# A hybrid decoder layer on one core: four edits, at the start, in the selection of experts, at the hand-over to v and in the final norm

## The chip, the cores and the metric

The kernel runs on one core of one Trainium2 chip. The metric is the device time of one execution in microseconds (us). The core has TensorE (PE, matmuls; PEld is its weight load), VectorE (DVE), ScalarE (ACT), GpSimd (POOL) and SyncE (SP), which here only issues DMAs. Each engine takes its instructions in the order in which they are written, and waits on semaphores for the others. A queue that issues DMAs does the same: a DMA that has to wait holds up all that stand behind it on its issuer.

## The reference

One trunk layer for 512 tokens of 1024 columns in float32:

```python
h = x + W_out [ GLA_group(n) ; SSD_group(n) ],   n = RMSNorm(x)
h = h + PEER(RMSNorm(h))
y = RMSNorm_final(h)
```

PEER is a retrieval of experts: per token 8 heads choose 16 of 16384 experts each by product keys, then

```python
act = jnp.einsum('td,ted->te', x_blk, u[i_blk])
hid = jax.nn.gelu(act, approximate=False) * g_blk
return jnp.einsum('te,ted->td', hid, v[i_blk])
```

## The kernel before, in words

The order of the work is written out by hand: the program sets no schedule of its own, so what stands first in the code stands first on its engine.

**Precision.** Most products are done in three matmuls (`mm3`, L106): an operand is split into a rounded high part, made by ACT, and the rest, made by DVE or POOL (`split`, L102), and high by high, high by low and low by high are added in PSUM (L108, L109, L110).

**Mixers** (`mixers`, L132). The four token tiles of x are loaded, squared, scaled by their norm (`scale`, L237), transposed on PE (L266), and evicted from PSUM as high part `nT` (ACT) and low part (DVE). Then the blocks of the input projection follow. `ahead` (L158) loads and splits weight blocks ahead of their use; raw blocks are `wraw`, split ones `b`. The first blocks' low parts are made by POOL.

**U steps.** PEER is done densely for three of the four token tiles (384 tokens, `TD`): for each of 128 blocks e of 128 experts, PE computes u of the block times the tokens (a U step: 8 parts of 3 matmuls of 384 columns, `u_part`, L1050), ACT applies gelu, and the result is kept in `ring`, 59 rows of 384 tokens. The raw block of u, `ur` (two buffers), is loaded by SP and split in two halves, one half-step ahead (`rhs_part`, L839). Before the gates are there, the halves' low parts `ul` are made by POOL, from `hold` on by DVE. The fourth tile's experts are gathered row by row by indirect DMAs (`gather`).

**Selection** (from L1086). While U steps run on PE, DVE picks the best experts: `select(t)` (L976) resolves token tile t to expert numbers with float16 comparisons and sums over `gat`; `ties(t)` (L962) lets ACT write four pieces of a helper tile `k` inside the following U steps, at parts 1 and 5; two tiles of `k` serve four t, so the pieces of t+2 wait until `select(t)` has read its last. `spread(t)` (L1013) transposes the numbers and the gates of tile t on PE, `spread2(t)` (L1022) moves them to float16. `u_run(n)` stands for n U steps.

**Gates** (from L1214). 48 units of 8 tokens each: DVE builds one-hot tiles `A`, `eq`, `B`, PE multiplies them (L1186), and the gates go by ACT and DVE to `ring` (rows that exist) or by ACT to `stage`, which every 8 units is written to DRAM, `gd`, by a DMA of ACT's queue (L1199). Between the units U parts are spread evenly: `parts = 8 * (RS - LEFT - nu[0])`, so that 57 U steps are done at the end, whatever number was done before.

**Hand-over and loop over v** (from L1230). The pool of the gates (`gp`) is closed and the pool of v (`vp`) opened on the same bytes: its raw buffers `vr` lie where `stage` lay. Then comes the loop over e (L1322): per turn 6 groups of 3 matmuls of 512 columns (v of block e times the ring row e, accumulated in 6 PSUM banks), one U step, two or one gathers, the loads of the next `vr`, `ur` and, once a row is used, of `ring` from `gd` (`gload`, L1251). From row 59 on the gate is in the ring row before the U step's result is multiplied into it by DVE (`keep`, L1036).

**Final norm** (`final`, L1257). For each tile the residual is added from PSUM (DVE), squared halfwise (ACT), the mean (two short DVE instructions) goes to POOL for the power -0.5, and the result is scaled by that and by the norm's weight.

Of the kernel before, what the change touches and what calls it, by code (L numbers as in the profile page):

```python
# [7 lines left out]
F32 = mybir.dt.float32  # L8
F32R = mybir.dt.float32r
# [9 lines left out]
D = 1024  # L19
# [16 lines left out]
class Stream:  # L36
# [10 lines left out]
    def loads(s, upto):  # L47
        while s.nl <= min(upto, len(s.src) - 1):
            s.raw[s.nl] = s.c.tile([128, 1024], F32, name=s.nm + "r", bufs=s.nraw)
            s.y.load(s.raw[s.nl], s.src[s.nl])  # L50
            s.nl += 1
# [12 lines left out]
class Layer:  # L64
# [67 lines left out]
    def mixers(self):  # L132
# [125 lines left out]
        scale(2, 1, False)  # L258
        scale(3, 0, True)
# [7 lines left out]
        for dc in range(8):  # L267
            if dc == 0:
                ahead(0, 3, 0)
            act(nh[dc], px[dc], AF.Copy, scale=wmix[:, dc:dc + 1])  # L270
            stt(nl[dc], px[dc], wmix[:, dc:dc + 1], nh[dc].bitcast(F32), OP.mult, OP.subtract)
            if dc == 4:
                ahead(0, 3, 1)
# [584 lines left out]
    def experts(self):  # L858
# [237 lines left out]
        select(1)  # L1096
        spread(0)
        u_run(1)
# [10 lines left out]
        u_run(4)  # L1109
# [124 lines left out]
        vs.loads(1)  # L1234
# [4 lines left out]
        vs.loads(3)  # L1239
# [15 lines left out]
        gload(RS)  # L1255

        def final():  # L1257
# [3 lines left out]
            junk = [c.tile([128, D], F32, name="gat", tag="gat", bufs=3), vp.tile([128, D], F32, name="vr", bufs=4)]  # L1261
# [26 lines left out]
            def scale(t):  # L1288
                stt(hs[t], hs[t], v[t][:, 3:4], wf, OP.mult, OP.mult)
                load(self.out[t], hs[t])  # L1290
# [9 lines left out]
            scale(3)  # L1300
            mean(0)
            power(0)
            residual(1, 0)
            weight(1, 0, G)
            residual(1, 1)
            weight(1, 1, G)
            scale(0)
            mean(1)
            power(1)
            residual(2, 0)  # L1310
            weight(2, 0, G)
            residual(2, 1)
            weight(2, 1, V)
            act(hs[1], hs[1], AF.Copy, scale=v[1][:, 3:4])
            load(self.out[1], hs[1])
            mean(2)
            power(2)
            act(hs[2][:, hf[0]], hs[2][:, hf[0]], AF.Copy, scale=v[2][:, 3:4])
            V.tensor_scalar(hs[2][:, hf[1]], hs[2][:, hf[1]], v[2][:, 3:4], None, op0=OP.mult)
            load(self.out[2], hs[2])  # L1320

        for e in range(NE):  # L1322
# [8 lines left out]
            vs.loads(e + 4)  # L1331
# [15 lines left out]
            for i in range(3):  # L1347
                vgrp(0, i)
                if i == 2:
# [3 lines left out]
                    gload(e + 1 + RS)  # L1353
# [3 lines left out]
            for i in range(3):  # L1357
# [5 lines left out]
                fill(3 + i)  # L1363
            u_part(7)
            fill(6)
            if e == NE - 12:
                for t in (0, 1):
                    hs[t] = us.c.tile([128, D], F32, name="ur", bufs=2)
# [100 lines left out]
```

## Time and profile before

| what | before |
|---|---|
| median of 3 runs | 1508.53 us |
| lowest and highest of them | 1506.76 and 1512.19 us |
| the profiled execution, its time | 1503.02 us |
| span of the profiled execution, first to last instruction | 1501.2 us |
| busy share of the span: PE, DVE, ACT, POOL | 97%, 78%, 42%, 30% |
| DMA: mean rate over the span | 224 GB/s |

The profiled execution's own time is 1.8 us longer than its span, which is launch and end around it; it lies 0.4% under the median of the three runs. Engines work side by side, so a busy share says little by itself: what counts is where PE, the busiest engine, stands still, and what ended each stop. A matmul row gives the start and the modelled duration; matmuls are pipelined, so the pace is read from start to start. In the rows further below, the bracket at the end is the engine's idle time before the instruction and what ended it.

### The profile page before, as it was taken

How to read it: one execution, taken by the hardware profiler on the slowest of the kernel's cores; microseconds unless marked ns; L12 is line 12 of the kernel's file. 1: busy time of each engine (PE TensorE's matmuls, PEld its weight loads, DVE VectorE, ACT ScalarE, POOL GpSimd, SP SyncE). 2: the span in 40 equal slices, each digit the busy share in tenths (PEclk: the TensorE clock that was granted, in tenths of full speed). 3: DMA queues.
4: the chain of work that ended last, by engine and by line, in shares of the span. 5: the costliest groups of instructions: out<-in, count | busy, mean ns of one | idle time of the engine just before them, and what ended most of it. 6: DMA issues, size and time to landing. Idle time of an engine off the chain costs nothing.

```text
span 1501.2 us, 22402 instructions
## 1 busy us (share of the span) xinstructions
PE 1456.2 (97%) x7904; PEld 1278.0 (85%) x7904; DVE 1169.4 (78%) x2473; ACT 632.7 (42%) x1201; POOL 451.7 (30%) x380
## 2 busy tenths in 40 slices
PE   7999999999898999979999999999999999999997
PEld 5787778888898999878999999999999998888886
DVE  6542663789999999967877778777788888888886
ACT  5435633433654544433333333333333333444444
POOL 2002404444672000002333333333333333333332
PEclk9999999999999999999999999999999999999999
DMA  5231224222334556658888888889899888888894
GB/s 189 84 126 58 71 73 155 96 85 85 105 104 143 159 167 175 180 181 300 322 316 316 323 312 307 317 305 332 304 331 322 314 316 276 292 300 299 297 325 178
DMA packets 148738, 335.56 MB, mean 224 GB/s; under 512 B 64640, under 2 KB 73872, under 8 KB 148496
## 3 DMA queue, kind: packets, MB, share of 16 engines
q1 hardware_dynamic: 58672, 186.32, 36.1%
q0 software_dynamic: 36864, 134.23, 25.1%
q10 hardware_dynamic: 53088, 13.57, 3.9%
q8 instruction: 62, 1.02, 0.3%
q14 instruction: 52, 0.43, 0.1%
HBM read 315.79 MB, written 18.28 MB: 223 GB/s over the span
## 4 chain that ended last, share of the span: by engine, by line
PE 80%; DVE 12%; issue 3%; DMA 2%; ACT 2%; POOL 0%; SPq 0%; DVEq 0%; POOLq 0%; ACTq 0%
PE pm L109 25%; PE pm L108 25%; PE pm L110 25%; DVE gat L97 4%; PE pg L1186 2%; DVE B L97 1%; DVE ul L104 1%; PE pm L904 1%; DMA gd<-stage 1%; DVE ring L97 1%; DMA ur<-in_uT 1%; DVE eq L97 1%; DVE A L97 1%; ACT b L91 0%; ACT tp L91 0%
## 5 line engine op out<-in xcount | busy, mean ns | idle before, releaser
L108 PE MATMUL pm<-nT,uh 128*128 128x384 f32 (+1 forms) x1152 | 402.1, 349 | 8.8 <-ACT uh L91 8.3
L110 PE MATMUL pm<-nT,ul 128*128 128x384 f32 (+1 forms) x1152 | 397.0, 345 | 2.0 <-POOL ul L104 2.0
L109 PE MATMUL pm<-nT,uh 128*128 128x384 f32 (+1 forms) x1152 | 397.0, 345 | 0.5 <-DVE nT L97 0.5
L109 PE MATMUL pm<-vl,hh 128*128 128x512 f32 x765 | 300.4, 393 | 0.2 <-DVE vl L104 0.2
L110 PE MATMUL pm<-vh,hl 128*128 128x512 f32 x765 | 300.3, 393 | 0.0
L108 PE MATMUL pm<-vh,hh 128*128 128x512 f32 x765 | 299.0, 391 | 0.2 <-ACT vh L91 0.2
L1135 POOL DMA_INDIRECT gat<-in_u,idx x128 | 136.8, 1069 | 473.3 <-DVE gat L100 467.0
L91 ACT ACTIVATE uh<-ur 128x512 fp32r<-128x512 f32 x288 | 180.2, 629 | 214.1 <-PE pm L109 182.0
L108 PEld LDWEIGHTS pm<-nT,uh 128*128 128x128 f32 x1152 | 218.1, 189 | 33.5 <-ACT uh L91 8.7
L109 PEld LDWEIGHTS pm<-nT,uh 128*128 128x128 f32 x1152 | 218.1, 189 | 25.0 <-DVE nT L97 1.1
L110 PEld LDWEIGHTS pm<-nT,ul 128*128 128x128 f32 x1152 | 217.7, 189 | 9.1 <-POOL ul L104 2.9
L1135 POOL DMA_INDIRECT gat<-in_v,idx x128 | 147.2, 1150 | 253.1 <-DVE n2a L100 220.4
L91 ACT ACTIVATE vh<-vr 128x512 fp32r<-128x512 f32 x255 | 159.4, 626 | 136.8 <-PE pm L110 135.4
L104 DVE TENSOR_TENSOR vl<-vr,vh 128x512 fp32r<-128x512 f32 x255 | 175.3, 688 | 37.4 <-ACT vh L91 36.4
L104 DVE TENSOR_TENSOR ul<-ur,uh 128x512 fp32r<-128x512 f32 x206 | 140.7, 689 | 56.8 <-ACT uh L91 56.4
L100 DVE SCALAR_TENSOR_TENSOR n2a<-gat,dots,n2a 128x1024 f32<-128x1024 f32 x128 | 164.0, 1281 | 21.5 <-DMA gat<-in_v,idx 18.5
L110 PEld LDWEIGHTS pm<-vh,hl 128*128 128x128 f32 x765 | 143.7, 188 | 30.9
L100 DVE SCALAR_TENSOR_TENSOR gat<-gat,n2a 128x1024 f32<-128x1024 f32 x128 | 156.2, 1220 | 9.8 <-DMA gat<-in_u,idx 9.6
L108 PEld LDWEIGHTS pm<-vh,hh 128*128 128x128 f32 x765 | 144.0, 188 | 14.2 <-ACT vh L91 0.7
L109 PEld LDWEIGHTS pm<-vl,hh 128*128 128x128 f32 x765 | 144.0, 188 | 14.1 <-DVE vl L104 0.5
L104 POOL TENSOR_TENSOR ul<-ur,uh 128x512 fp32r<-128x512 f32 x82 | 118.7, 1455 | 99.8 <-ACT uh L91 99.4
L91 ACT ACTIVATE gl<-pm 128x384 f32<-128x384 f32 (+16 forms) x104 | 46.0, 442 | 219.8 <-PE pm L110 219.8
(254 smaller groups left out, 1685.2 us busy)
## 6 DMA issues: line engine op xcount, KB each, us to landing
ur<-in_uT SPq DMA_DIRECT2D x128, 512.0 KB, 6.0
vr<-in_v SPq DMA_DIRECT2D x128, 512.0 KB, 5.0
gd<-stage ACTq DMA_DIRECT2D x6, 2208.0 KB, 14.5
ring<-gd SPq DMA_DIRECT2D x69, 192.0 KB, 5.2
wraw<-in_w_in SPq DMA_DIRECT2D x23, 512.0 KB, 4.4
ur<-in_w_query SPq DMA_DIRECT2D x16, 512.0 KB, 3.7
b<-in_x SPq DMA_DIRECT2D x8, 512.0 KB, 3.6
wraw<-in_w_out SPq DMA_DIRECT2D x8, 512.0 KB, 3.9
```

What stands on the lines that cost most here:

```text
L91: return self.S.activation(out, in_, f, **k)
L97: return self.V.tensor_tensor(out, x, y, op=op)
L100: return self.V.scalar_tensor_tensor(out, x, s, y, op0=op0, op1=op1, **k)
L104: (self.G if pool else self.V).tensor_tensor(lo, src, hi.bitcast(F32), op=OP.subtract)
L108: T.matmul(out, lhi, rhi, start=start, stop=False)
L109: T.matmul(out, lhi, rlo, start=False, stop=False)
L110: T.matmul(out, llo, rhi, start=False, stop=stop)
L904: T.matmul(p[:, t * 128:(t + 1) * 128], q[:, t * 128:(t + 1) * 128], skT[:, b, :], start=True, stop=True)
L1135: G.indirect_dma_start(out=r, out_offset=None, in_=src, in_offset=bass.IndirectOffsetOnAxis(ap=idx[:, k:k + 1], axis=0))
L1186: T.matmul(o, A[:, t // 2, :, t % 2], B[:, i, t // 2, :, t % 2], start=i == 0, stop=i == 1)
```

## The change

The change has four parts.

1. Raw buffers. The buffers of a `Stream` (raw u and raw v) get a name each (`ur0`, `ur1`, `vr0` to `vr3`) where one name with several buffers stood. With that the four buffers of v are taken in the order in which they are first loaded, in rising addresses: `vr0` to `vr2` lie in the bytes of the one `stage` buffer, `vr3` across its border to the other. Three blocks of v are loaded ahead of the loop where four were, in one go; the fourth with the two next in turn 1. The loads of ring rows 59 and 60 from `gd` move from ahead of the loop and from turn 0's start to the end of turn 0.
2. Selection. `spread(0)` stands behind two U steps where it stood behind none, and one U step stood after it; the last run of U steps has five in place of four. In all 20 U steps lie in this stretch where 18 lay, and two fewer in the gates.
3. Start. The first weight block is split ahead of the last scaling of x, in halves, its low part by POOL; the third `wraw` load ahead stands one eviction later.
4. Final norm. Scalings are halved and put in another order, two multiplications by the weight on POOL fall away, and the last tile's output goes out in two halves, from ACT's and from SP's queue.

```diff
@@ Stream.loads
-            s.raw[s.nl] = s.c.tile([128, 1024], F32, name=s.nm + "r", bufs=s.nraw)
+            s.raw[s.nl] = s.c.tile([128, 1024], F32, name=f"{s.nm}r{s.nl % s.nraw}", bufs=1)
@@ mixers
         scale(2, 1, False)
+        parts[0] = b4(F32R), b4(F32R)
+        for k in range(2):
+            f = slice(k * 512, k * 512 + 512)
+            act(parts[0][0][:, f], raws[0][:, f], AF.Copy)
+        for k in range(2):
+            f = slice(k * 512, k * 512 + 512)
+            self.G.tensor_tensor(parts[0][1][:, f], raws[0][:, f], parts[0][0][:, f].bitcast(F32), op=OP.subtract)
+        raws.pop(0)
+        seen[1] = 1
         scale(3, 0, True)
...
-            if dc == 0:
+            if dc == 1:
                 ahead(0, 3, 0)
@@ experts, selection
         select(1)
+        u_run(2)
         spread(0)
-        u_run(1)
         ties(3)
...
         spread(2)
-        u_run(4)
+        u_run(5)
         spread2(2)
@@ experts, hand-over
-        vs.loads(1)
+        vs.loads(2)
         u_run(1)
         vs.split(1)
         hprep(0)
         u_run(1)
-        vs.loads(3)
...
-        gload(RS)
@@ final
...
             residual(1, 0)
             weight(1, 0, G)
+            scale(0, hf[0])
             residual(1, 1)
-            weight(1, 1, G)
-            scale(0)
+            residual(2, 0)
+            scale(0, hf[1])
+            load(self.out[0], hs[0])
+            residual(2, 1)
             mean(1)
             power(1)
-            residual(2, 0)
-            weight(2, 0, G)
-            residual(2, 1)
-            weight(2, 1, V)
-            act(hs[1], hs[1], AF.Copy, scale=v[1][:, 3:4])
-            load(self.out[1], hs[1])
+            scale(1, hf[1])
             mean(2)
             power(2)
+            act(hs[1][:, hf[0]], hs[1][:, hf[0]], AF.Copy, scale=v[1][:, 3:4])
+            load(self.out[1], hs[1])
+            weight(2, 0, V)
             act(hs[2][:, hf[0]], hs[2][:, hf[0]], AF.Copy, scale=v[2][:, 3:4])
-            V.tensor_scalar(hs[2][:, hf[1]], hs[2][:, hf[1]], v[2][:, 3:4], None, op0=OP.mult)
-            load(self.out[2], hs[2])
+            self.S.dma_start(self.out[2][:, hf[0]], hs[2][:, hf[0]])
+            scale(2, hf[1])
+            load(self.out[2][:, hf[1]], hs[2][:, hf[1]])
@@ experts, loop over e
-            vs.loads(e + 4)
+            vs.loads(e + 4 if e else 2)
...
-                    gload(e + 1 + RS)
+                    if e:
+                        gload(e + 1 + RS)
...
+            if e == 0:
+                gload(RS)
+                gload(RS + 1)
             u_part(7)
```

SP's queue at the hand-over, before. `vr` are raw blocks of v, `ur` of u, `ring<-gd` rows of gates; the brackets name the semaphores that a DMA waits for.

```order
L88 DMA vr_6961<-in_v 128x1024 [waits DMAHW6_49,PE_49]
L88 DMA vr_6963<-in_v 128x1024 [waits DMAHW4_49,Activation_49]
L88 DMA ur_6966<-in_uT 128x1024 [waits DMAHW2_49,DVE_49]
L88 DMA ur_7012<-in_uT 128x1024 [waits DMAHW3_49,DVE_49]
L88 DMA vr_7049<-in_v 128x1024
L88 DMA vr_7051<-in_v 128x1024
L88 DMA ring_2196<-gd_64 128x384 [waits DVE_49]
```

The same place in the change:

```order
L88 DMA vr0_6957<-in_v 128x1024 [waits DMAHW6_49,PE_49]
L88 DMA vr1_6959<-in_v 128x1024
L88 DMA vr2_6961<-in_v 128x1024
L88 DMA ur1_6964<-in_uT 128x1024 [waits DMAHW2_49,DVE_49]
L88 DMA ur0_7010<-in_uT 128x1024 [waits DMAHW3_49,DVE_49]
L88 DMA ur1_7061<-in_uT 128x1024 [waits DMAHW0_49,DVE_49]
L88 DMA ring_2198<-gd_64 128x384 [waits DMAHW4_49]
```

The wait for DMAHW4 stood on the second load of v, ahead of two loads of u; now it stands on the first ring row, behind three loads of v and three of u.

ACT's queue in the selection around `spread(0)`, before. A row `ring<-pm` ends a U step, `uh` are halves of u, `k8` pieces of `ties`, `gs` belongs to `spread(0)`.

```order
L91 ACTIVATE ring_2196<-pm_3859 128x384 [waits PE_49]
L91 ACTIVATE gs_2210<-pm_3912 128x128 [waits PE_49]
L91 ACTIVATE uh_3920<-ur_3860 128x512 [waits DMAHW2_49,Pool_49]
L91 ACTIVATE k8_3858<-tif_2205 128x1024
L91 ACTIVATE uh_3937<-ur_3860 128x512 [waits PE_49,Pool_49]
L91 ACTIVATE k8_3858<-tif_2205 128x1024
L91 ACTIVATE ring_2196<-pm_3917 128x384 [waits PE_49]
L91 ACTIVATE uh_3974<-ur_3918 128x512 [waits DMAHW3_49,Pool_49]
L91 ACTIVATE k8_3955<-tif_2205 128x1024 [waits DVE_49]
L91 ACTIVATE uh_3991<-ur_3918 128x512 [waits PE_49,Pool_49]
```

In the change:

```order
L91 ACTIVATE ring_2198<-pm_3861 128x384 [waits PE_49]
L91 ACTIVATE uh_3917<-ur1_3862 128x512 [waits DMAHW2_49,Pool_49]
L91 ACTIVATE k8_3860<-tif_2207 128x1024
L91 ACTIVATE uh_3934<-ur1_3862 128x512 [waits PE_49,Pool_49]
L91 ACTIVATE k8_3860<-tif_2207 128x1024
L91 ACTIVATE ring_2198<-pm_3914 128x384 [waits PE_49]
L91 ACTIVATE uh_3955<-ur0_3915 128x512 [waits DMAHW3_49,Pool_49]
L91 ACTIVATE uh_3971<-ur0_3915 128x512 [waits PE_49,Pool_49]
L91 ACTIVATE ring_2198<-pm_3952 128x384 [waits PE_49]
L91 ACTIVATE gs_2212<-pm_3988 128x128 [waits PE_49]
L91 ACTIVATE uh_4012<-ur1_3953 128x512 [waits DMAHW4_49,Pool_49]
L91 ACTIVATE k8_3993<-tif_2207 128x1024 [waits DVE_49]
```

The piece of `ties(3)` that waits for DVE stands in the second U step after `spread(0)` before, and in the first one after it now; a U step without pieces lies ahead of `spread(0)`.

DVE's queue in the final norm, before, from the second half of tile 1's residual. `ur` are tiles 0 and 1, `gat` with `pm` tile 2, `rs3` the norms' small numbers, `gat_14506` the weight.

```order
L100 SCALAR_TENSOR_TENSOR ur_14224<-pm_7060,ur_14224 128x512 [waits PE_49]
L100 SCALAR_TENSOR_TENSOR ur_14222<-ur_14222,rs3_14554,gat_14506 128x1024 [waits Pool_49]
L1282 TENSOR_SCALAR rs3_14555<-rs3_14555 128x1 [waits Activation_49]
L1283 TENSOR_SCALAR rs3_14555<-rs3_14555 128x1 [waits DVE_49,Activation_49]
L100 SCALAR_TENSOR_TENSOR gat_14508<-pm_7061,gat_14508 128x512 [waits DMAHW3_49,PE_49]
L100 SCALAR_TENSOR_TENSOR gat_14508<-pm_7062,gat_14508 128x512 [waits PE_49]
L1279 TENSOR_TENSOR gat_14508<-gat_14508,gat_14506 128x512 [waits Activation_49]
L1282 TENSOR_SCALAR rs3_14556<-rs3_14556 128x1
L1283 TENSOR_SCALAR rs3_14556<-rs3_14556 128x1 [waits DVE_49]
L1319 TENSOR_SCALAR gat_14508<-gat_14508,rs3_14556 128x512 [waits Pool_49]
```

In the change:

```order
L100 SCALAR_TENSOR_TENSOR ur1_14220<-pm_7054,ur1_14220 128x512 [waits PE_49]
L100 SCALAR_TENSOR_TENSOR gat_14504<-pm_7055,gat_14504 128x512 [waits DMAHW3_49,PE_49]
L100 SCALAR_TENSOR_TENSOR ur0_14218<-ur0_14218,rs3_14550,gat_14502 128x512
L100 SCALAR_TENSOR_TENSOR gat_14504<-pm_7056,gat_14504 128x512 [waits PE_49]
L1288 TENSOR_SCALAR rs3_14551<-rs3_14551 128x1 [waits Activation_49]
L1289 TENSOR_SCALAR rs3_14551<-rs3_14551 128x1 [waits DVE_49,Activation_49]
L100 SCALAR_TENSOR_TENSOR ur1_14220<-ur1_14220,rs3_14551,gat_14502 128x512 [waits Pool_49]
L1288 TENSOR_SCALAR rs3_14552<-rs3_14552 128x1 [waits Activation_49]
L1289 TENSOR_SCALAR rs3_14552<-rs3_14552 128x1 [waits DVE_49,Activation_49]
L1285 TENSOR_TENSOR gat_14504<-gat_14504,gat_14502 128x512
L100 SCALAR_TENSOR_TENSOR gat_14504<-gat_14504,rs3_14552,gat_14502 128x512 [waits Pool_49]
```

Both residuals of tile 2 now stand ahead of tile 1's mean, a scaling of tile 1 that waits for POOL stands ahead of tile 2's mean, and the weighting of tile 2 behind it.

## Rows read from the trace of the kernel before

**Rows 1.** Busy time by stretch: us, then PE, PEld, DVE, ACT, POOL, PEclk, DMA share, GB/s.
```profile
15.00:215.00 200.00, 199.08 (x1052) 154.88 (x1053) 108.17 (x198) 97.13 (x163) 33.87 (x15) 0.99 0.27 88
...
680.00:1484.00 804.00, 804.00 (x3912) 709.92 (x3911) 643.40 (x960) 308.07 (x583) 277.96 (x251) 1.00 0.88 308
```
**Rows 2.** Same view: spread(0), the first unit, the early units, the late units, hand-over.
```profile
408.86:417.02 8.16, 4.17 (x16) 3.71 (x15) 7.92 (x10) 3.62 (x7) 3.45 (x3) 0.79 0.28 93
462.60:468.87 6.27, 5.83 (x34) 5.54 (x34) 4.52 (x8) 2.08 (x4) 1.76 (x2) 0.73 0.78 253
468.87:559.14 90.27, 89.17 (x748) 84.88 (x747) 86.00 (x161) 46.06 (x109) 0.00 (x0) 1.00 0.49 143
559.14:654.09 94.95, 91.32 (x750) 85.70 (x750) 93.81 (x166) 44.46 (x111) 1.15 (x1) 1.00 0.58 165
667.39:680.02 12.63, 4.37 (x13) 3.65 (x14) 4.39 (x8) 2.98 (x6) 0.61 (x1) 0.59 0.90 318
```
**Rows 3.** PE's waits over the span: us in total, times, longest.
```profile
PE pg L1186 <- DVE B L97: 8.6, 18, 3.3
```
**Rows 4.** The timeline of the start: start, us, engine, instruction, idle before it.
```profile
11.93 0.72 ACT L91 ACTIVATE b<-b,rs 128x512 f32<-128x512 f32 x1 [1.22 <-POOL rs L235]
...
12.55 1.04 ACT L91 ACTIVATE b<-wraw 128x1024 fp32r<-128x1024 f32 x1
...
16.09 0.50 PE L110 MATMUL pm<-nT,b 128*128 128x512 f32 x1 [0.35 <-POOL b L104]
```
**Rows 5.** PE's timeline at spread(0) and in the U step behind it.
```profile
411.74 0.33 PE L1017 MATMUL pm<-ident,ii 128*128 128x128 f32 x1 [2.62 <-DVE ii L97]
...
417.19 0.34 PE L108 MATMUL pm<-nT,uh 128*128 128x384 f32 x1
417.36 0.34 PE L109 MATMUL pm<-nT,uh 128*128 128x384 f32 x1
```
**Rows 6.** The group of one DVE product in the selection: ns least/median/most, first to last.
```profile
L97 DVE TENSOR_TENSOR gat<-gat,k x5: 1224/2125/2130, 398.4 to 427.1; 128x2048 f16<-128x2048 f16 x5
```
**Rows 7.** The group of POOL's low parts of u, the same columns.
```profile
L104 POOL TENSOR_TENSOR ul<-ur,uh x82: 1264/1294/2288, 237.4 to 457.9; 128x512 fp32r<-128x512 f32 x82
```
**Rows 8.** ACT's waits, 405 to 430 us: total, times, longest.
```profile
ACT k L91 <- DVE gat L97: 3.4, 2, 2.5
```
**Rows 9.** The page's costliest groups: DVE's low parts of u, busy us, mean ns.
```profile
L104 DVE TENSOR_TENSOR ul<-ur,uh 128x512 fp32r<-128x512 f32 x206 | 140.7, 689 | 56.8 <-ACT uh L91 56.4
```
**Rows 10.** The timeline of SP at the hand-over.
```profile
652.55 17.66 SPq L88 DMA_DIRECT2D vr<-in_v  x2
```
**Rows 11.** The waits of SP's queue, 600 to 700 us.
```profile
SPq L88 <- DMA gd<-stage: 16.9, 1, 16.9
```
**Rows 12.** The timeline of DVE, ACT and PE at the hand-over.
```profile
657.78 0.69 DVE L104 TENSOR_TENSOR ul<-ur,uh 128x512 fp32r<-128x512 f32 x1 [0.66 <-ACT uh L91]
...
674.97 1.15 ACT L91 ACTIVATE uh<-ur 128x512 fp32r<-128x512 f32 x2 [10.46 <-DMA ur<-in_uT]
...
675.65 0.69 PE L108 MATMUL pm<-nT,uh 128*128 128x384 f32 x1 [8.26 <-ACT uh L91]
```
**Rows 13.** The page's DMA issues: count, KB each, median us to landing.
```profile
gd<-stage ACTq DMA_DIRECT2D x6, 2208.0 KB, 14.5
ring<-gd SPq DMA_DIRECT2D x69, 192.0 KB, 5.2
```
**Rows 14.** The group of tile ur, 460 to 700 us: its loads' time to landing.
```profile
DMA to landing us min/median/max: 3.5/4.2/7.0
```
**Rows 15.** The timeline of the final norm's end.
```profile
1495.01 1.40 POOL L1279 TENSOR_TENSOR gat<-gat 128x512 f32<-128x512 f32 x1
...
1495.39 0.21 DVE L1283 TENSOR_SCALAR rs<-rs 128x1 f32<-128x1 f32 x1
1496.38 0.54 POOL L1286 TENSOR_TENSOR rs<-rs,mhalf 128x1 f32<-128x1 f32 x1
...
1497.70 0.33 SPq L88 DMA_DIRECT2D out_dram<-gat  x1
```

More of the change, by code (lines that the diff above doesn't have):

```diff
@@ L1260, in final @@
             hf = [slice(0, 512), slice(512, 1024)]
-            junk = [c.tile([128, D], F32, name="gat", tag="gat", bufs=3), vp.tile([128, D], F32, name="vr", bufs=4)]
+            junk = [c.tile([128, D], F32, name="gat", tag="gat", bufs=3), vp.tile([128, D], F32, name=f"vr{NE % 4}", bufs=1)]
             v = [nv() for _ in range(4)]
@@ L1286, in power, with scale @@
                 G.tensor_tensor(v[t][:, 3:4], v[t][:, 0:1], self.mhalf, op=OP.pow)
-            def scale(t):
-                stt(hs[t], hs[t], v[t][:, 3:4], wf, OP.mult, OP.mult)
-                load(self.out[t], hs[t])
+            def scale(t, cols=slice(0, D)):
+                stt(hs[t][:, cols], hs[t][:, cols], v[t][:, 3:4], wf[:, cols], OP.mult, OP.mult)
             square(3, 0)
@@ L1300, in final @@
             scale(3)
+            load(self.out[3], hs[3])
             mean(0)
@@ L1367, in experts @@
                 for t in (0, 1):
-                    hs[t] = us.c.tile([128, D], F32, name="ur", bufs=2)
+                    hs[t] = us.c.tile([128, D], F32, name=f"ur{t}", bufs=1)
                     load(hs[t], self.hd[t])
```

## The prediction

> **What bounds the kernel now.** I read the busy time by stretch first, to see where PE, the busiest engine, is not busy, then PE's waits, then the timeline and SP's waits at each stop. PE works without a stop through the mixers and through the whole loop over v, 804 of 804 us [rows 1]: there, time moves only with the number of matmuls, and a stretch that begins earlier ends earlier by as much. The stops lie at four places, and each part of the change stands at one of them. At the start the first matmul with a low part of the weights comes at 16.09 us, and POOL's low part is what it waited for [rows 4]. In the selection DVE is the bound: PE waits for `spread(0)` and, at the stretch's end, 3.3 us for the first one-hot product [rows 3, 5]. In the gates both engines are nearly full: in the early units PE is busy 89.2 of 90.3 us, in the late ones DVE 93.8 of 95.0 [rows 2]. At the hand-over PE stands still for 8.26 us [rows 12], the longest stop behind the first loads; it begins at 675.65 - 8.26 = 667.4.
>
> A U step is 24 matmuls, and at full clock one of 384 columns follows another in 0.17 us [rows 5], so a step is 4.16 us of PE, and a part of three matmuls 0.52. For other widths I scale the pace by the columns: 0.23 us for 512, 0.06 for 128.
>
> **The hand-over.** SP issues two loads of v over 17.66 us, the second at the end of that time [rows 10], and SP's longest wait there is 16.9 us for the last store of `stage` [rows 11]. The load itself is not urgent. But the next raw block of u stands behind it on SP: ACT gets that block 10.46 us late, and PE waits for the split half [rows 12]. In the change the first three blocks of v lie off that buffer; the wait goes to the ring row, behind the loads of u. What is late next? The u block's own buffer is free when its second half is split, at 657.78 + 0.69 = 658.5 us [rows 12]; with the longest landing seen while stores ran, 7.0 us [rows 14], it is there at 665.5, and PE asks for the split half at 667.4. The two added loads of v (1 MB) pass ahead of it on the same queue; I allow 0.4 us for that, with 0 and 1.5 as ends. The stop also cost clock: behind it TensorE's granted clock was low, 0.59 over the stretch with its idle time, and the 13 matmuls up to 680.02 took 4.37 us [rows 2], where 6 at 0.17 and 6 or 7 at 0.23 take 2.4. So the part gives 8.26 + 1.9 - 0.4 = **9.8 us**, ends 8.3 and 10.2.
>
> The ring row's wait must be paid by someone. Before, the last store had landed when SP issued the second load, at 652.55 + 17.66 - 0.33 = 669.9 [rows 10]; with more loads beside it I take 671.5. The row lands 5.2 later [rows 13], at about 676.7. `keep` for row 59 stands at the end of turn 0 on DVE and needs it; I estimate it due at 675.5, two U steps behind 667.4, so DVE waits about a microsecond. What stands behind it on DVE is a gather's product and the low part of a u half that PE wants a turn later, some 8 us on. I cost it at nothing.
>
> **Selection.** Two U steps more are 8.3 us of PE. They fill what PE now loses: 408.86 to 417.02 holds 16 matmuls, 2.6 us at full clock, so 5.5 of the 8.16 us are waits and the low clock behind them [rows 2], and 3.3 us lie idle before the first unit [rows 3]. By PE alone the gates would start 0.5 us earlier. DVE pays, though. One product there takes 1.22 us or 2.13, the long ones beside a POOL instruction [rows 6]: 0.9 us per meeting. Two steps bring four more POOL low parts [rows 7], so up to 4 x 0.9 = 3.6 us on DVE's path. And a wait moves: the piece of `ties(3)` that waits for `select(1)`, 2.5 us on ACT now [rows 8], stands one U step nearer to `spread(0)`. Before, its step begins 11 matmuls behind 417.02, at 418.9; in the change two U steps and `spread(0)`'s three short matmuls behind 408.86, at 408.86 + 8.3 + 0.5 = 417.7, while `select(1)` ends no earlier and, beside the added POOL work, perhaps 0.4 later. Behind it on ACT is the u half that PE needs next, which now arrives just in time, so PE loses 1.2 + 0.4 = 1.6 us. While it waits POOL is idle and DVE runs free, so the two prices do not add. I take **+1.6 us** for the start of the gates, ends -0.5 and +3.6.
>
> The Trainium skill, page "SBUF — State Buffer", section "SBUF: two separate sides", says that DVE and GpSimd share one pair of ports as an exclusive lock, held for a whole instruction. By it each of the four POOL instructions (1.29 us median, 2.29 at most [rows 7]) could hold DVE for its full length, 5.2 us; the trace agrees on the lock but shows 0.9 us a meeting [rows 6].
>
> **Gates.** The 3.3 us stop also leaves the first unit at a low clock: 6.27 us for 34 matmuls at 0.73 [rows 2], where 18 at 0.17 and 16 at 0.06 make 4.0. PE is idle for 0.44 of it (6.27 - 5.83); the rest, 1.8 us, comes back if PE arrives busy: **-1.8**. Then 31 U steps lie among 48 units in place of 33: 16 parts less. Where PE is the bound that is 16 x 0.52 = 8.3 us. Where DVE is, it is four low parts at 0.69 [rows 9] and two products of the ring, smaller tiles, so no more than 0.69 each: 6 x 0.69 = 4.1 us. PE holds the early half, DVE the late one [rows 2]: the mean, **-6.2 us**, with 4.1 and 8.3 as ends. These steps are done in the selection in any case, so nothing is lost of the work.
>
> **Start.** ACT idles 1.22 us before the last scaling [rows 4]; one of the split's two halves, 1.04 / 2 = 0.5 us each, ends there, so the last scaling moves little and the evictions behind it begin 0.5 us earlier, while POOL's low part is done before PE asks: 0.5 and the 0.35 that PE waited for it [rows 4], about 1 us in all with what is late behind it. The block's landing is not shown before 12.55, when ACT reads it at once; if it lands only then, nothing is won and the last scaling is late by 0.5. I take **-1.0**, ends +0.5 and -1.1. PE is full from there on [rows 1].
>
> **Final norm.** Tile 2's power waits on POOL behind the weighting: the mean ends at 1495.60, the power starts at 1496.38 [rows 15], 0.8 us lost. The change takes that multiplication away, but puts a scaling of tile 1 ahead of tile 2's mean on DVE, which costs back about half of it. **-0.4**, ends -1.2 (the 0.8 and a halved output) and +0.5 (a half scaling too late on DVE, about what a low part of that size takes [rows 9]).
>
> The other edits (names of raw u buffers, order of the third weight load) move no wait that I can find: 0.
>
> Sum: -9.8 + 1.6 - 1.8 - 6.2 - 1.0 - 0.4 = **-17.6 us** against the profiled execution's 1503.02, which is 5.5 us under the median of the runs. Taken off the median, 1508.53, it gives **1490.9 us**. All terms at their good ends make -10.2 - 0.5 - 1.8 - 8.3 - 1.1 - 1.2 = -23.1, all at their bad ends -8.3 + 3.6 - 1.8 - 4.1 + 0.5 + 0.5 = -9.6: 1485.4 and 1498.9.
>
> **Rivals.** (a) The hand-over's wait only moves. The store's packets and three loads of v keep the DMA engines full (0.90 behind the stop [rows 2]) and the u block lands 5 us later than I assume. PE then stops some 4.5 us, and loses clock too: -9.8 becomes about -4, **1496.7**. Against it: 7.0 us was the most while stores ran [rows 14].
> (b) What the gates win, the selection gives back: each POOL low part holds DVE for 5.2 / 4 = 1.3 us [rows 7] in place of 0.9, and the piece of `ties(3)` holds PE on top of it, 1.2 us; with the gates at their DVE end that makes 5.2 + 1.2 - 1.8 - 4.1, about nothing in place of -6.4: **1497.3**. For it: DVE's path sets this stretch. This is the page's rule in full.
> (c) The names do not change where the buffers lie, and SP still waits. Then only the rest is left: -7.8, **1500.7**. The queue as listed speaks against it, since the second and third load of v carry no wait.
> (d) Slower: the ring row. `keep` of row 59 blocks DVE until the row has landed, and all splits stand behind it. PE has about 8 us of split work in hand from 675.5. To undo 17.6 us and make 4.5 more, PE must stop for 22.1, so the row must land at 675.5 + 8 + 22.1 = 705.6 or later, in place of 676.7; then **1513** or more. The store's and the row's landings [rows 13] put it far off.
>
> **How the numbers follow.** Forecast 0.70, (a) 0.12, (b) 0.11, (c) 0.03, (d) 0.03, and 0.01 for what I have not seen. The forecast's own range is 1487 to 1496, since not all terms go to one end together; the low end stands, and (a), (b) and the spread of the runs shown, 2.7 us to either side of their middle, carry the high end to 1500.5. A measurement of this kernel tells about 0.3%, 4.5 us, from no change, so faster means under 1504.0. The forecast, (a), (b) and (c) lie there, 0.96, of which I move 0.03 to no change for (c) with a poor start and norm. With the 0.01 that makes faster 0.93, within it 0.04, slower 0.03.
>
> **What would show it.** In the profile of the change: the second load of v issued within a microsecond of the first; PE's longest stop at the hand-over under 2 us, and no low clock behind it; no PE wait at `spread(0)`, but one of 1 to 3 us in the U step behind it; the first unit of the gates at full clock; the 48 units in about 183.5 us in place of 654.09 - 462.60 = 191.5 [rows 2]; `ring<-gd` first issued at about 664 to 666 us, earlier by what was won before; POOL's low part of the first weights ended before PE asks for it; the last tile's power not held behind a weighting on POOL. I am wrong if PE still stops over 4 us at the hand-over, or if the gates begin over 4 us later and take no less time.

## The result, and the profile after

| | before | changed |
|---|---|---|
| median of 4 runs | 1507.87 us | 1493.07 us |
| lowest and highest | 1506.76, 1512.19 us | 1490.10, 1494.82 us |
| profiled execution, its time and span | 1503.02, 1501.2 us | 1490.10, 1488.3 us |

The ratio of the runs is 0.9895, 95% interval 0.9869 to 0.992: 15.8 us less (12.1 to 19.8); the two medians differ by 14.8. A later set of runs of the changed kernel, with its own runs of before, gave 0.9879 (0.9844 to 0.9913). The forecast was 1490.9 us. The total came out; the stages show that three of its terms did not.

Busy time by stretch in the changed kernel, columns as in [rows 1]: the two U steps ahead of `spread(0)` with its three short matmuls, first unit, early units, late units, hand-over. They answer to [rows 2].

```profile
408.50:417.00 8.50, 8.50 (x52) 8.47 (x51) 8.26 (x10) 6.03 (x11) 4.64 (x4) 1.00 0.42 132
465.22:469.86 4.64, 4.26 (x34) 3.97 (x34) 4.22 (x8) 2.06 (x4) 3.28 (x3) 1.00 0.84 260
469.86:557.20 87.34, 85.72 (x723) 80.83 (x723) 84.94 (x157) 44.17 (x105) 0.00 (x0) 1.00 0.51 152
557.20:651.85 94.65, 89.35 (x743) 82.94 (x743) 93.85 (x166) 42.32 (x107) 1.14 (x1) 1.00 0.59 167
662.67:671.00 8.33, 8.33 (x44) 7.54 (x44) 6.14 (x11) 3.21 (x6) 1.15 (x1) 1.00 0.99 278
```

PE runs through `spread(0)` and through the hand-over at a granted clock of 1.00, and the first unit has its full clock too. In the U step behind `spread(0)` PE does wait in this profile, 1.5 us for a high half of u (the row `PE pm L108 <- ACT uh` below), as forecast; the second profile of the same kernel (`a_again`) has no such stop. PE's waits over the span (line, releaser, total us, times, longest):

```profile
PE pg L1195 <- DVE B L97: 7.9, 23, 1.1
...
PE pm L110 <- POOL ul L104: 2.8, 3, 1.6
PE pm L108 <- ACT uh L91: 1.5, 1, 1.5
PE pm L1026 <- DVE ii L97: 1.3, 1, 1.3
```

The 8.26 us of [rows 12] and the 3.3 us of [rows 3] are gone. SP's queue at the hand-over (start, us, and how many DMAs are merged into a row):

```profile
648.70 1.33 SPq L88 DMA_DIRECT2D vr<-in_v  x3
654.64 8.71 SPq L88 DMA_DIRECT2D ur<-in_uT  x3
669.61 0.80 SPq L88 DMA_DIRECT2D ring<-gd  x2
```

Three loads of v go out within 1.33 us where two took 17.66 [rows 10], three of u follow, and the wait for the store ends only at the ring row.

Since all profiles of this study have the same instructions in a stretch that its kernel leaves alone, the stretches can be read several times, each from one named instruction to another, by their starts; the last one-hot product and the last product with `vh` (three with `uh` follow it) count by their ends. Before: the first profile, a second one of the same kernel (`b_again`), and the hand-over part alone (`e1_hand`). Changed: where a mean stands, all profiles that have the stretch as the change has it; otherwise the first profile of the change, and the second (`a_again`) behind it.

| stretch | before, us | changed, us | difference | forecast |
|---|---|---|---|---|
| start: first transpose to the 200th projection matmul (`pm<-nT,b`) | 88.26, 88.47, 87.67 | 87.55, mean of 11 (86.98 to 88.23) | -0.6 | -1.0 |
| selection: first U step to first one-hot product | 221.38, 220.67, 220.77 | 224.76, mean of 8 (224.28 to 225.78) | +3.8 | +1.6 |
| first unit of the gates | 6.26, 6.27, 5.89 | 4.64 (first profile) | -1.5 | -1.8 |
| the other 47 units | 186.85, 186.81, 186.59 | 182.05, mean of 6 | -4.7 | -6.2 |
| hand-over: last one-hot product to the first product of turn 1 | 29.50, 29.48 | 19.14, 19.13 | -10.4 | -9.8 |
| rest of the loop over v | 807.04, 807.11 | 807.93, 807.05 | +0.4 | 0 |
| last product to the end | 8.99, 8.97, 8.97 | 9.38, in both | +0.4 | -0.4 |

Together that is -12.6 us; the first two profiles differ by 1501.24 - 1488.30 = 12.94. The loop is the row to be careful with: in six more profiles that have the changed kernel's loop unaltered it takes 808.7 to 815.8 us (see "What stays open").

The whole selection in the same view, before and in the change, columns as above:

```profile
241.23:462.61 221.38, 209.95 (x1106) 189.57 (x1107) 187.62 (x889) 98.84 (x163) 119.68 (x92) 0.99 0.32 105
240.38:465.22 224.84, 217.29 (x1153) 196.70 (x1154) 191.05 (x889) 101.64 (x169) 124.25 (x95) 1.00 0.33 106
```

DVE has the same 889 instructions in both, and is busy 3.4 us longer.

### The profile page after: what moved, and what is told of

It is laid out like the page before. It is cut to its first block, busy times and chain, and to the rows that moved or that the text cites. A ratio compares the mean times of both kernels' runs of the same rounds, so it can differ in the third digit from the quotient of the medians.

```text
span 1488.3 us, 22407 instructions
## 1 busy us (share of the span) xinstructions
PE 1454.3 (98%) x7904; PEld 1275.2 (86%) x7904; DVE 1171.2 (79%) x2469; ACT 632.2 (42%) x1200; POOL 457.2 (31%) x383
## 4 chain that ended last, share of the span: by engine, by line
PE 81%; DVE 12%; issue 3%; ACT 2%; DMA 1%; POOL 0%; POOLq 0%; DVEq 0%; SPq 0%; ACTq 0%
PE pm L109 25%; PE pm L108 25%; PE pm L110 25%; DVE gat L97 4%; PE pg L1195 2%; DVE B L97 1%; DVE ul L104 1%; DVE eq L97 1%; DVE ring L97 1%; DVE A L97 1%; PE pm L913 1%; ACT b L91 0%; ACT tp L91 0%; PE pm L275 0%; DVE tp L97 0%
## 5 line engine op out<-in xcount | busy, mean ns | idle before, releaser
L108 PE MATMUL pm<-nT,uh 128*128 128x384 f32 (+1 forms) x1152 | 400.4, 348 | 2.0 <-ACT uh L91 1.5
L108 PE MATMUL pm<-vh,hh 128*128 128x512 f32 x765 | 298.6, 390 | 0.2 <-ACT vh L91 0.2
L108 PEld LDWEIGHTS pm<-nT,uh 128*128 128x128 f32 x1152 | 216.6, 188 | 26.4 <-ACT uh L91 1.8
L100 DVE SCALAR_TENSOR_TENSOR n2a<-gat,dots,n2a 128x1024 f32<-128x1024 f32 x128 | 163.8, 1279 | 20.5 <-DMA gat<-in_v,idx 17.1
L108 PEld LDWEIGHTS pm<-vh,hh 128*128 128x128 f32 x765 | 143.7, 188 | 14.3 <-ACT vh L91 0.7
L104 POOL TENSOR_TENSOR ul<-ur,uh 128x512 fp32r<-128x512 f32 x86 | 124.5, 1455 | 100.4 <-ACT uh L91 99.3
L91 ACT ACTIVATE gl<-pm 128x384 f32<-128x384 f32 (+15 forms) x102 | 45.4, 445 | 220.5 <-PE pm L110 220.5
```

Source lines behind the costliest of these rows:

```text
L91: return self.S.activation(out, in_, f, **k)
L100: return self.V.scalar_tensor_tensor(out, x, s, y, op0=op0, op1=op1, **k)
L104: (self.G if pool else self.V).tensor_tensor(lo, src, hi.bitcast(F32), op=OP.subtract)
L108: T.matmul(out, lhi, rhi, start=start, stop=False)
```

## The experiments

**The hand-over part alone** (`e1_hand`): the kernel before with these edits of the change.

```diff
-            s.raw[s.nl] = s.c.tile([128, 1024], F32, name=s.nm + "r", bufs=s.nraw)
+            s.raw[s.nl] = s.c.tile([128, 1024], F32, name=f"{s.nm}r{s.nl % s.nraw}", bufs=1)
...
-        vs.loads(1)
+        vs.loads(2)
...
-        vs.loads(3)
...
-            vs.loads(e + 4)
+            vs.loads(e + 4 if e else 2)
```

(with the two other names, and `gload(RS)` and `gload(RS + 1)` at the end of turn 0.)

> The kernel before with the hand-over part of the change alone (names of the raw buffers, loads of v, place of the first ring rows). Theory A (the part is worth by itself what the trace of the change shows between the last one-hot product and the loop, -10.4 us): ratio to before about 0.993, PE's stop of 8.3 us gone, start, selection and gates as before. Rival B (it is worth that only because the change also ends the gates sooner, or the wait only moves to the ring row and comes back in turn 0): at most 6 us, ratio 0.996 or more, with a new PE stop of 3 us or more behind turn 0.

Measured: 1494.30 us against 1511.35, ratio 0.9914 (0.9887 to 0.9942). Its hand-over takes 19.14 us, to a hundredth what it takes in the change, and PE does not wait there at all. Theory A holds; the upper end of the interval, 0.9942, leaves no room for rival B's 0.996. By the runs the part is worth 13.0 us (8.8 to 17.1), which takes in the stage's 10.4.

**The change without its hand-over part** (`e2_rest`): the same edits, turned round, on the changed kernel.

> The changed kernel with its hand-over part undone. Theory A (the other three parts are worth what the milestones of the two traces show: start -0.85, selection +3.5, first unit -1.6, other gates -4.9, end +0.4): -3.5 us, ratio about 0.998, and PE's 8.3 us stop at the hand-over is there as before. Theory P (the prediction's terms: -1.0 +1.6 -1.8 -6.2 -0.4): -7.8 us, ratio 0.995. Rival C (the two U steps are worth nothing, what the gates win is lost in the selection): ratio 0.9995 to 1.000.

Measured: 1508.25 us against 1511.35, ratio 0.9979 (0.996 to 0.9998), 3.2 us less. Theory A's 0.998; the forecast's 0.995 lies outside. Rival C's 0.9995 lies just inside, so the runs alone do not rule it out; the stages of this profile speak against it, 3.3 us lost in the selection and 6.2 won in the gates. With `e1_hand` the two halves make 13.0 + 3.2 = 16.2 us, against 15.8 for the whole. PE's wait at the hand-over is back:

```profile
PE pm L108 <- ACT uh L91: 8.5, 1, 8.5
```

**Names without the order of the loads** (`e3_names`): the changed kernel with `vs.loads(1)`, `vs.loads(3)`, `vs.loads(e + 4)` and both `gload` where they were.

> The changed kernel with the names of the raw buffers kept, but the loads of v and the ring rows issued where they were before. SP then holds two loads of v, two of u, two more of v of which the last waits for the store, a ring row, and only then the third load of u. Theory A (what counts is how many loads of u stand ahead of the wait for the store): the long stop at the hand-over is gone, but the third u block comes some 6 to 7 us later than in the change, and PE stops 3 to 6 us one turn later: 3 to 7 us above the change. Rival (the addresses alone do it): within 1.5 us of the change.

Measured: 1502.91 us against 1511.35, ratio 0.9952 (0.9929 to 0.9974); by ratios 8.6 us above the change. SP's timeline and PE's waits from 650 to 700 us:

```profile
654.22 3.53 SPq L88 DMA_DIRECT2D ur<-in_uT  x2
657.80 11.80 SPq L88 DMA_DIRECT2D vr<-in_v  x2
669.64 0.43 SPq L88 DMA_DIRECT2D ring<-gd  x1
670.12 0.43 SPq L88 DMA_DIRECT2D vr<-in_v  x1
670.65 0.38 SPq L88 DMA_DIRECT2D ur<-in_uT  x1
```

```profile
PE pm L108 <- ACT hh L91: 2.5, 1, 2.5
PE pm L109 <- DVE vl L104: 1.0, 1, 1.0
```

The long stop is gone by the names alone: two blocks of u pass ahead of the load that waits. But the third is issued 19.2 us behind the last one-hot product (670.65 - 651.43) where the change issues it 11.2 behind (663.03 - 651.85), after three DMAs that went out within 1.4 us before it; ACT, held by it, is late with what stands behind it. The stops themselves are 3.5 us, but the clock falls behind them, to 0.73 in the second full turn of the loop:

```profile
681.57:694.12 12.55, 11.51 (x43) 9.93 (x43) 11.26 (x20) 4.07 (x8) 4.45 (x4) 0.73 0.73 253
```

The first two full turns take 11.00 and 12.55 us and the later ones 8.44, so stops and clock together cost 6.7 us, the high end of theory A; the turn itself is longer too in this profile (below).

**Ring rows where they were** (`e4_ring`): the changed kernel with `gload(RS)` ahead of the loop and `gload(e + 1 + RS)` in turn 0.

> The changed kernel with only the two first ring rows loaded where they were before, so that the first, with its wait for the store, stands ahead of the third load of u. Theory A: the third u block is issued when the store has landed, about 670 us instead of 663, and lands about 675.5, where ACT asks for it at 671.6: PE stops 2 to 5 us and loses some clock, 2 to 6 us above the change. Rival (the place of the ring rows is worth nothing): within 1.5 us of the change.

Measured: 1493.32 us, ratio 0.9897 (0.9868 to 0.9926). SP's timeline:

```profile
652.58 3.52 SPq L88 DMA_DIRECT2D ur<-in_uT  x2
666.63 0.33 SPq L88 DMA_DIRECT2D ring<-gd  x1
667.05 0.38 SPq L88 DMA_DIRECT2D ur<-in_uT  x1
```

Theory A falls here. The third block of u is issued 17.3 us behind the last one-hot product (667.05 - 649.79), 6.1 later than in the change, next in line behind one ring row; yet the view of PE's waits lists none from 650 to 700 us, and the hand-over takes 19.13 us. So there were over 6 us in hand for that block, and the ring row is not what costs in `e3_names`. What is left there are the last 2 us, the fuller queue and the other order of the loads of v; no run takes these apart. So the new place of the ring rows, a part of the change, is worth nothing that shows here.

**One U step fewer and one more in the selection** (`e5_run4`, `e5_run6`).

```diff
-        u_run(5)
+        u_run(4)
```

```diff
-        u_run(5)
+        u_run(6)
```

> The changed kernel with four U steps in the selection's last run, as before, in place of five (so 32 U steps among the gates instead of 31). Theory L (each POOL low part holds DVE, which sets the selection's end): from the first U step to the first one-hot product 1.9 us less than in the change (224.84), about 222.9; the gates behind the first unit, 181.99 us in the change, 2.3 us more. Rival PE (the selection's end is set by PE's matmuls and ACT's order): 4.2 us less, about 220.7.

> The changed kernel with six U steps in the selection's last run in place of five (30 among the gates). Theory L: from the first U step to the first one-hot product 1.9 us more than in the change, about 226.8, as long as PE has idle time left there, and the gates behind the first unit 2.3 us less, about 179.7: the two together -0.4 us. Rival PE (PE's matmuls set the end by now): 4.2 us more, about 229.0, and the two together +1.9 us.

Each ran once, in 1498.50 and 1493.72 us, in executions whose loops differ by 5.2 us, so the stages are read instead:

| U steps | selection | first unit | other units | sum |
|---|---|---|---|---|
| 4 | 222.50 | 6.27 | 183.36 | 412.13 |
| 5 (first profile; means of the table above) | 224.84; 224.76 | 4.64 | 181.99; 182.05 | 411.47; 411.45 |
| 6 | 227.60 | 3.59 | 181.19 | 412.38 |

From four to five the selection grows by 2.3 us, a little over theory L's 1.9 and far from 4.2. From five to six it grows by 2.8, between the two theories: PE has no wait left there for the first one-hot product, so PE now shares the bound. The gates give back 2.9 and then 1.9. Five is the best of the three, by 0.7 to 0.9 us, less than runs can tell and less than the 1.5 us over which the selection of the change itself ranges.

**The waiting piece one U step later** (`e6_ties`).

```diff
         spread(0)
+        u_run(1)
         ties(3)
         select(2)
-        u_run(2)
+        u_run(1)
```

> The changed kernel with one of the two U steps that stand between select(2) and spread(1) put between spread(0) and ties(3), so that the piece that waits for select(1) comes a U step later on ACT. ACT's wait of 5.6 us for it falls to 2 us or less, and PE's stops behind spread(0) (1.5 us for a high half, 1.6 for a low one) go. Theory L (DVE sets the stretch's end, PE's stops there are idle time): the first one-hot product comes at the same time within 0.5 us, 224.8 us behind the first U step. Theory P (the prediction: the piece holding PE is what the stretch loses): 1.6 to 3 us earlier.

ACT's wait for the piece, in the change and here:

```profile
ACT k L91 <- DVE gat L97: 6.6, 2, 5.6
```

```profile
ACT k L91 <- DVE gat L97: 2.7, 1, 2.7
```

One of the two waits is gone; the one that is left, 2.7 us, misses the 2 us expected. PE's 1.5 us stop for a high half falls to 0.3. Yet the first one-hot product comes 224.28 us behind the first U step, within the change's 224.28 to 225.78: theory L. The comparison with the first profile is weaker than it looks, though, since six of the eight profiles with the change's selection have that stop at 0 to 0.3 us without this edit. They say the same from their side: `a_again`, with no such stop, has a selection of 225.04 us against 224.84 with it.

**Another end of the final norm** (`e7_tail`).

```diff
             mean(1)
-            power(1)
+            weight(2, 0, V)
+            mean(2)
+            G.tensor_tensor(w2[:, :, 3:4], w2[:, :, 0:1], bc(self.mhalf, 1, 2), op=OP.pow)
...
+            load(self.out[2], hs[2])
```

(`w2` holds the small numbers of tiles 1 and 2; then ACT and DVE scale half of tile 1 each, and of tile 2.)

> The changed kernel with another end of the final norm: one power for the means of tiles 1 and 2 together, the weighting of tile 2 on DVE ahead of the second mean and not beside the power, and tile 2 written by one DMA. Theory L (a DVE product beside it makes POOL's power 0.93 us in place of 0.54, and the last output in two halves lands 0.4 us later than in one): last v matmul to the end 9.38 us in the change becomes about 8.4. Rival (the end is set by the DMAs alone, the power's length is chance): 9.0 to 9.4.

Measured: 9.33 us from the last product to the end, the rival's figure (its one run, 1496.95 us, has a long turn of the loop). The timeline of the change, then of this kernel:

```profile
1482.50 0.68 DVE L1285 TENSOR_TENSOR gat<-gat 128x512 f32<-128x512 f32 x1
1482.66 0.93 POOL L1292 TENSOR_TENSOR rs<-rs,mhalf 128x1 f32<-128x1 f32 x1 [1.25 <-DVE rs L1289]
1483.62 0.72 ACT L91 ACTIVATE gat<-gat,rs 128x512 f32<-128x512 f32 x1 [1.45 <-POOL rs L1292]
...
1484.38 0.40 ACTq L1326 DMA_DIRECT2D out_dram<-gat  x1
1484.40 0.33 SPq L88 DMA_DIRECT2D out_dram<-gat  x1
```

```profile
1488.75 0.70 POOL L1321 TENSOR_TENSOR rs<-rs,mhalf 128x2 f32<-128x2 f32 x1 [2.60 <-DVE rs L1290]
...
1490.97 0.33 SPq L88 DMA_DIRECT2D out_dram<-gat  x1
```

The last output goes out 5.13 us behind the last product in place of 5.48, but tile 1's output was issued only 0.64 us earlier, and the last one took 3.3 us to land, where a whole tile alone took 2.6 in `e8_bact` below. What the engines won, the two transfers side by side gave back. The first half of theory L is not refuted: in all ten profiles that have the change's norm the last power lasts 0.92 or 0.93 us beside DVE's product, in the three of the old norm 0.54 with no DVE instruction beside it, and here, with none either, 0.70 for two columns.

**A bound taken off the late units** (`e8_bact`, `e9_bact2`), beside the changed kernel once more (`a_again`) and the kernel before once more (`b_again`).

```diff
-            for i in range(2):
-                tt(B[:, i], eq, two(gs[:, i, w]), OP.mult)
+            tt(B[:, 0], eq, two(gs[:, 0, w]), OP.mult)
+            q = UT // 2 - (LATE if u >= NU // 2 else 0)
+            tt(B[:, 1, :q], eq[:, :q], two(gs[:, 1, w])[:, :q], OP.mult)
...
+                    act(late[0][0], late[0][1], AF.Copy, scale=late[0][2])
...
-            self.S.dma_start(self.out[2][:, hf[0]], hs[2][:, hf[0]])
             scale(2, hf[1])
-            load(self.out[2][:, hf[1]], hs[2][:, hf[1]])
+            load(self.out[2], hs[2])
```

(`late` lists the tokens left to ACT; `LATE` is 1 or 2 pairs of them a unit.)

> The changed kernel once more, unaltered, beside the next ones and for a second profile. The stretches from the start to the loop over v as in the first profile within 0.5 us each (first U step to first one-hot product 224.3 to 224.9, gates behind the first unit 182.0, last one-hot product to the loop's first full turn 19.14, end 9.4). Open: whether a turn of the loop takes 8.32 us again (then the pace goes with the kernel) or one of the longer paces seen in other runs, 8.39 or 8.44 (then it goes with the execution).

> The changed kernel with two edits more. In the last 24 units of the gates ACT makes a quarter of the second one-hot product (two tokens, two short instructions with one token's low gate part, copied once to float32, as the scale), DVE three quarters; and tile 2 of the output goes out in one DMA. Theory L (DVE is the bound of the late units, and PE has room): 0.15 us less DVE per unit, the last 24 units about 91 us in place of 94.65. Rival (ACT's order becomes the bound there, or PE's 89.4 us of work and its waits do): 94 us or more. End: 9.0 us behind the last v matmul if the two halves cost 0.4, 9.4 if not.

> The same with half of the second one-hot product made by ACT (four tokens, four instructions a unit) in the last 24 units. Theory L: DVE is 0.3 us a unit shorter, PE's own 89.4 us become the bound, so 89.5 to 91 us for them. Rival: ACT, four instructions of some 0.2 us later in each unit, holds the next unit's first matmul or the next half of u, and the stretch is longer than with two.

> The kernel before once more, unaltered, for a second profile. First U step to first one-hot product 220.8 to 221.4, hand-over 29.4 to 29.5 us, end 9.0; a turn of the loop 8.32 us again if the pace goes with the kernel, 8.39 or 8.44 in place of it if it goes with the execution.

Measured against 1509.85 us of before: `a_again` 1491.69, ratio 0.9879 (0.9844 to 0.9913); `e8_bact` 1491.14, ratio 0.9878 (0.9841 to 0.9916); `e9_bact2`, one run, 1488.37; `b_again`, one run, 1502.53. Busy time of the last 24 units with two and with four tokens on ACT, and ACT's group of these products:

```profile
557.53:649.97 92.44, 89.16 (x743) 82.88 (x743) 91.09 (x166) 57.00 (x155) 1.15 (x1) 1.00 0.60 170
```

```profile
558.24:649.70 91.46, 89.82 (x743) 83.48 (x743) 88.53 (x165) 70.90 (x203) 1.14 (x1) 1.00 0.61 174
```

```profile
L91 ACT ACTIVATE B<-eq,g 128x128 f16<-128x128 f16 x96 | 34.4, 436 | 8.7 <-DVE eq L97 8.7
```

DVE goes from 93.85 to 91.09 and 88.53 us, the stretch from 94.65 to 92.44 and 91.46: it follows DVE first, then PE's 89.8 us. That is theory L, with both stretches a little above its figures (about 91, and 89.5 to 91); at 436 ns each the products cost ACT twice what I had reckoned, and it had the room. The end is 9.06 and 9.05 us with one output DMA. By its stages `e9_bact2` stands 3.2 + 0.3 = 3.5 us under the change, and its span, 1486.6 us, is the shortest of all profiles; its one run can't show so little, and `e8_bact` and `a_again` are the same by theirs.

## Why the prediction was right, and where it was not

**Hand-over, -9.8: right.** No load of u waits for the store; the one that I gave 7.0 us, issued at 654.64, is read by ACT 6.4 us later, and the next, issued at 657.84, landed 7.1 us later; PE does not stop and keeps its clock. The measured -10.4 is 0.2 beyond the end of 10.2, so the allowance of 0.4 for the two added loads was too much. (The other end was added up wrong: 8.26 + 1.9 - 1.5 is 8.7, not 8.3.) The mechanism was the one argued, and `e1_hand` shows that the part needs no other. One step inside it was wrong: the ring row would be issued at 664 to 666 us "earlier by what was won before". It was 669.61, because the store, issued at 652.63, held the row for 17.0 us in place of the 13.4 of before (656.49 to 669.88). The load that waits for that store goes out 13.3 to 13.4 us behind it in the three profiles with the old hand-over, and 16.1 to 19.0 us behind it in the eleven others, in which loads of u and v go out beside it. DVE waited 2.0 us for the row, I had said 1, and the reason why that is free (a turn of split work in hand) held.

**Selection, +1.6: mis-sized, measured +3.8, just beyond its end of 3.6.** The step that failed is "PE loses 1.2 + 0.4 = 1.6 us" as the value taken. I had two prices, 3.6 us on DVE's path and 1.6 on PE's, and since they do not add I took the smaller; where two paths run side by side the longer one counts, and I had myself named DVE as the bound. PE's price was no price: in six of eight profiles its stop is 0 to 0.3 us, and their selection takes 224.28 to 225.06 us against the first one's 224.84. DVE's price can be counted. Set side by side instruction by instruction, DVE's work from its first top-16 search on is the same 881 instructions in every profile; 14 or 15 of them last about 1.0 us longer than their shortest in the three profiles of before, 18 or 19 in the eight with the change's selection, 16 in `e5_run4`, and each of them ran beside a POOL low part of u (not every meeting costs: the float32 top-16 searches meet them by the hundred and none is long). Four more long ones at 1.0 us make the 3.8. The rule of the Trainium skill, page "SBUF — State Buffer", section "SBUF: two separate sides", gave 5.2 us for the same four; the measurement decides for 1.0 a meeting, close to my 0.9. In `e5_run6` 19 are long, only one more than in most, so most of its 2.8 us points to PE's side.

**First unit, -1.8, measured -1.5: right.** Clock 1.00 in place of 0.73. `e5_run4` shows whose work it is: with four U steps PE waits again and the unit takes 6.27 us.

**Other units, -6.2, measured -4.7: inside its ends (4.1 and 8.3), but the wrong mean.** The late half gave 96.57 - 94.65 = 1.9 us (half of DVE's 4.1), as DVE as a bound asks. (The row of the late units in [rows 2] ends 1.6 us ahead of the last one-hot product, so 96.57 stands here for its 94.95.) The early half gave 90.27 - 87.34 = 2.9, not 4.2: there PE was taken as the bound throughout, but with fewer U parts its own busy time falls by 3.5 while its idle time grows from 1.1 to 1.6; why the busy time falls by 3.5 and not by 8 x 0.52 = 4.2 is open. `e9_bact2` shows that DVE holds the late half.

**Start, -1.0, about -0.6.** PE's wait for the low part is gone, as forecast. Profiles with the new start range over 1.25 us and those with the old one over 0.8, and they overlap; the size stays open within that.

**Final norm, -0.4, measured +0.4: wrong sign.** The wait that I priced (0.8 us behind POOL's weighting) did go, and the power starts 0.37 us earlier, at 3.75 in place of 4.11 us behind the last product. But the change puts DVE's weighting at 1482.50 beside it, and the power lasts 0.93 in place of 0.54; the output is issued at the same 5.4 to 5.5 us. I had moved the weighting off POOL and not asked what DVE does beside the power. The halved output then costs 0.3: 9.38 against 9.06 us with one DMA.

**The total** agrees better than its terms: -17.6 forecast, -15.8 in the runs, -12.6 in the stages. The stages compare profiles in which the loop has its shortest turn; the runs hold longer ones too, which the prediction did not know of. Part of the agreement is therefore luck.

**What stays open.** The loop's turn has more than one length for the same instructions. From 720 to 1060 us, in the change, in `e2_rest` and in `b_again`:

```profile
720.00:1060.00 340.00, 340.00 (x1719) 307.86 (x1718) 269.34 (x459) 127.72 (x246) 115.67 (x108) 1.00 0.90 316
```

```profile
720.00:1060.00 340.00, 340.00 (x1693) 306.45 (x1692) 265.32 (x453) 124.97 (x242) 112.99 (x105) 1.00 0.87 311
```

```profile
720.00:1060.00 340.00, 340.00 (x1719) 307.83 (x1718) 268.79 (x460) 125.88 (x245) 116.15 (x108) 1.00 0.90 318
```

A turn is 42 matmuls: 340 / 1719 x 42 = 8.31 us, and 8.43 in `e2_rest`, with PE busy throughout and the clock granted in full. Over the 68 or so turns with U steps that is 8 us. Both profiles of before have the short turn, and both are near the shortest runs (1502.5 to 1516.7 in all sets); most runs of before, with a median of 1507.9 to 1511.4, lie 5 to 9 us above, those of the change 2 to 3 us above its first profile. That would fit a long turn being more frequent in the kernel before and would explain runs that differ by more than the stages, but only the profiled executions show their turns. PE's stop is not the rule behind it: `e2_rest` and `e3_names` stop and have the long turn, both profiles of before stop and have the short one, `e5_run4` has the long one without a stop.

Two things narrow it down. The difference lies in every matmul of a turn: in the long one of 8.44 us those of 384 columns follow one another in 177 ns in place of 173 and those of 512 in 233 in place of 231, while the turns without a U step take 4.08 us in all profiles. And the turn changes inside an execution: `e4_ring`, `e5_run6`, `e6_ties` and `e8_bact` have 8.32 us up to turn 48 and 8.44 from turn 50 on. In turn 49 DVE waits in every profile, 2.0 to 5.3 us, for a load into a buffer that is read until just before (`n2a`, where the fourth token tile's sum begins); in `e8_bact`:

```profile
DVE n2a L100 <- DMA n2a<-hd: 5.3, 1, 5.3
```

That turn takes 8.32 us in the first profile of before and in `a_again`, where PE does not stop, and up to 12.63 in `e7_tail`, where PE waits 2.5 us for a low part of v. Neither kernel does anything about this wait. Why the turn goes on longer behind it in four profiles and not in the others is open.

## What to carry to other kernels

A load that is in no hurry can hold one that is: look at which bytes a new buffer takes over, whose last reader (here a store of 17 us) it must wait for, and what stands behind it on the issuing queue; two addresses and one deferred load were worth 10 of the 13 us. When an edit lays a price on two engines that run side by side, take the longer path, not the smaller number. And when an operation leaves one engine for another, ask what the second engine's neighbours pay: a tiny instruction on the path took 1.7 times as long beside a wide one.

## What the runs showed of the hardware

In the final norm a POOL power of one column takes 0.54 us alone and 0.93 beside a 0.68 us DVE product of 128x512 in float32, in all ten profiles that have them side by side. In the selection 14 to 19 DVE instructions of a profile, nearly all on float16 tiles, last 0.88 to 1.14 us longer than their shortest, each beside one of POOL's float32 subtractions of 128x512 (1.29 us median); the float32 top-16 searches beside the same subtractions do not. From the last output's issue to the end of the program it is 3.5 us with one DMA of 512 KB on SP's queue, 4.2 with another such DMA 0.64 us ahead of it (`e7_tail`), and 3.9 with two of 256 KB on ACT's and SP's, though the halves landed no later than 2.75 us. And PE can run the same loop of matmuls at 8.32, 8.39 (`e7_tail`) or 8.44 us a turn without a wait and at the same granted clock; which one it takes differs from one execution to the next and can change within one, and no run here showed what decides it.
